# Conditioning sums of every second block on VectorE instead of TensorE, in a decoder layer

## The chip, the cores and the metric

The kernel runs on one core of a Trainium2 chip. The metric is the time of one execution on the device in microseconds; of several runs the median counts. The core has a matrix engine (TensorE, PE in the profile, with its weight loads listed as PEld), a vector engine (VectorE, DVE), a scalar engine (ScalarE, ACT), GpSimd (POOL) and a queue engine (SyncE, SP) that issues the transfers from memory here. Each engine takes its instructions in a fixed order and waits on semaphores for the others.

## The reference, cut to what matters

One decoder layer with two attention branches. The change touches only its beginning, the modulated norm and the first product with the input projection:

```
mod = silu(c) @ w_ada + b_ada                       # c: 1024 numbers, w_ada: 1024 x 3072
shift, scale, gate = split(mod, 3)
h = rms_norm(x, g_pre) * (1 + scale) + shift        # x: 256 tokens x 1024
proj = h @ w_in                                     # queries, keys, values and more
```

Behind it come two attentions, two output projections with gates, a merge, `w_out`, a second norm and the residual sum. They are the same before and after.

## The kernel before

Everything is in fp32, with 128 partitions. The 1024 channels are cut into eight blocks j = 0 to 7 of 128 channels. The first stage computes h of one block after the other (transposed, channels on partitions, tokens along the row) and at once multiplies it with the block's 128 rows of the input projection, 1536 columns, into six PSUM banks that collect over all eight blocks (two `acc` banks for queries, two `sc` for keys, two `pv` for values). For precision, h and the weights w are each split into a rounded part and a rest, and three products are formed: P0 = h1 w1, P1 = h2 w1, P2 = h1 w2. So each block has nine pairs of matmuls, P0q, P0k, P0v, P1q and so on, each pair for two tiles of 128 tokens.

To have h of block j, the kernel needs shift and scale of that block's 128 channels: a sum over all 1024 numbers of silu(c), with a slice of w_ada of 128 x 2048 numbers (8 slices k of 256 columns: 128 for shift, 128 for scale). The kernel makes it so:

- A (`ada_rows`, line 172): eight TensorE matmuls with a 32-column stationary operand (`scp`, silu(c) in its first column), that leave four rows of partial sums in the PSUM bank `bR` (tag `tr`). Behind them the slice's buffer `raw` is released, which lets SyncE issue the next load.
- E (`ada_evac`, line 181): ScalarE copies the 256 columns to SBUF (`rws`).
- T (`ada_cols`, line 185): two TensorE matmuls with `rws` and a column of ones sum over the partitions and turn the row into a column, again in `bR`.
- B (`ada_ab`, line 191): two tiny VectorE instructions make the factor and the offset per channel (`ab`).
- H and F (`h_act`, `h_full`): ScalarE writes h1 (rounded) and h in full; h (`h_low`): VectorE subtracts, giving h2.
- s and d: one split of a 128x512 piece of the weights; s is ScalarE's rounding copy, d is VectorE's subtraction `raw - w1`, three of each per block. The last d of a block releases the weights' `raw` buffer.

The order is written out by hand. The string `STEP` (line 44) lists, for the step of block j, the nine P of block j, and between them the letters above for block j+1 (s and d as well):

```
STEP = "s P0q P0k P0v P1q A d E s P1k P1v d P2q T B H F h s d P2k P2v"
```

`tokens` (line 368) walks through it, and `ordered` (line 77) ties each instruction to the one before it on its engine, so that for TensorE (key "T"), VectorE ("V") and ScalarE ("A") the program order in this stage is that of the string. `START` prepares block 0, `LAST` is the step of block 7. Five `raw` buffers go round; loads are issued in the fixed order of `LOADS` (line 36) by SyncE whenever a buffer is released. GpSimd builds the rotary tables meanwhile, from about 15 to 45 us.

Of the kernel before, what the change touches and what calls it, by code (L numbers as in the profile page):

```python
# [10 lines left out]
FT = mybir.dt.float32  # L11
# [3 lines left out]
OP = mybir.AluOpType  # L15
# [3 lines left out]
P = 128  # L19
D = 1024  # L20
S = 256
H = 8
KT = D // P
# [16 lines left out]

START = "A E T B H s F d h s d s d"
STEP = "s P0q P0k P0v P1q A d E s P1k P1v d P2q T B H F h s d P2k P2v"
LAST = "P0v P1v P2v V P0q P0k P1q P2q P1k P2k"
POOL_LOW = []

# [14 lines left out]
def hybrid_layer_kernel(ctx: ExitStack, tc: tile.TileContext, x, cols, pos, cst, gpost, bgate,  # L62
# [4 lines left out]
    wk = ctx.enter_context(tc.tile_pool(name="wk", bufs=2))  # L67
# [4 lines left out]
    V = nc.vector  # L72
# [4 lines left out]
    def ordered(eng, f, *a, **k):  # L77

        if eng in last_ins:
            with tc.issue_after(last_ins[eng]):  # L80
                r = f(*a, **k)  # L81
        else:
            r = f(*a, **k)
        last_ins[eng] = r.ins
        return r

    def bank(tag):
        return ps.tile([P, 512], FT, name=tag)
# [16 lines left out]
    raws, got, w1s, w2s = {}, {}, {}, {}  # L105
# [20 lines left out]
    sc = sb.tile([P, 8], FT, name="sc")  # L126
# [39 lines left out]

    ROW, COL = 0, 256
    rws = {}  # L170

# [9 lines left out]
    def ada_evac(j):  # L181
        rws[j] = wk.tile([P, 256], FT, name="rws", tag="acc", bufs=2)
        ordered("A", act, rws[j], bR[:, ROW:ROW + 256], AF.Copy)

    def ada_cols(j):
        r = rws.pop(j)
        for i in range(2):
            ordered("T", mm, bR[:, COL + 8 * i + j:COL + 1 + 8 * i + j], r[:, i * P:(i + 1) * P], ones[:, 0:1],
                    start=False, stop=True, skip_group_check=True)
# [47 lines left out]
    def pump():  # L237
        while loads and (loads[0] in ('p', 'm') or held[0] < RAW or loads[0][0] in raws):
            if loads[0] in ('p', 'm'):
                with tc.issue_after(dl[-1]):  # L240
                    dl.append((nc.sync.dma_start(post, pos) if loads.pop(0) == 'p' else nc.sync.dma_start(mask, cst[:, 160:])).ins)
                continue
            raw(*loads.pop(0))

    def release():
        held[0] -= 1
        pump()

    def split_one():
        if not splits:  # L250
            return False
        u, key, c0, a, b = splits[0]
        if key not in raws or got.get(key, 2048) < c0 + b:
            return False
        if a == 0:
            i = order.index(u)
            if i >= RING and order[i - RING] not in finished:
                return False
            w1s[u] = rg.tile([P, 1024], FR, name="w1", bufs=RING)
            w2s[u] = rg.tile([P, 1024], FR, name="w2", bufs=RING)  # L260
        splits.pop(0)
        r = raws[key][:, c0 + a:c0 + b]
        w = key[0] == "w"
        free = lambda eng, f, *a, **k: f(*a, **k)  # L264
        o = ordered if w else free
        if u == ("w", 0, 0) and a == 0:
            o("V", V.tensor_copy, w1s[u][:, a:b], r)
        else:
            o("A", act, w1s[u][:, a:b], r, AF.Copy)
        rel = key != ("gate",) and (not splits or splits[0][1] != key)  # L270
        if w:
            subs.append((u, key, a, b, r, rel))
            return True
        eng = "G" if (order.index(u), a // 512) in POOL_LOW else "V"
        free(eng, dict(V=V, G=G)[eng].tensor_tensor, w2s[u][:, a:b], r, w1s[u][:, a:b], op=OP.subtract)
        if rel:
            release()
        return True
# [3 lines left out]
    def sub_one():  # L282
        u, key, a, b, r, rel = subs.pop(0)
        ordered("V", V.tensor_tensor, w2s[u][:, a:b], r, w1s[u][:, a:b], op=OP.subtract)
        if rel:
            release()
# [27 lines left out]
        mm(bV[0][:, :P], ones, ones, start=True, stop=True)  # L314
    for t in range(2):
        act(scr, xs[:, t, :], AF.Square, accum_out=ss[:, t:t + 1])
    bR = bank("tr")
    for t in range(2):
        V.tensor_scalar(rs[:, t:t + 1], ss[:, t:t + 1], 1.0 / D, EPS, op0=OP.mult, op1=OP.add)
        pw = G.tensor_tensor(rs[:, t:t + 1], rs[:, t:t + 1], mhalf[:, 0:1], op=OP.pow)  # L320
# [2 lines left out]
        for g in range(2):  # L323
# [4 lines left out]
            dst, src = xnT[:, 4 * g:4 * g + 4, t * P:(t + 1) * P], b.rearrange("p (k n) -> p k n", k=4)  # L328
# [27 lines left out]
    def proj(j, which, lst, hard=True):  # L356
        for b, t, o, n, u in lst:
            w1, w2 = w1s["w", j, u], w2s["w", j, u]
            assert not any(x[0] == ("w", j, u) and x[3] < o + n and o < x[4] for x in splits)
            assert which < 2 or not any(x[0] == ("w", j, u) and x[2] < o + n and o < x[3] for x in subs)  # L360
            ha, wa = ((h1, w1), (h2, w1), (h1, w2))[which]
            m = (ordered if hard else lambda e, f, *a, **k: f(*a, **k))("T", mm, b[:, :n], ha[:, j, t * P:(t + 1) * P], wa[:, o:o + n],
                   start=(j == 0 and which == 0),
                   stop=(j == KT - 1 and which == 2), skip_group_check=True)
        return m.ins


    def tokens(j, toks):
        for t in toks.split():
            if t == "s":  # L370
                if splits[0][1][0] == "w":
                    assert split_one(), splits[0]
            elif t == "d":
                if subs:
                    sub_one()
            elif t[0] == "P":
                proj(j, int(t[1]), dict(q=accs[:2], k=accs[2:4], v=accs[4:])[t[2]])
            elif t == "V":
                vevac()
            elif j + 1 < KT:  # L380
                dict(A=ada_rows, E=ada_evac, T=ada_cols, B=ada_ab, H=h_act, F=h_full, h=h_low)[t](j + 1)

    tokens(-1, START)
    with tc.issue_after(pw.ins):
        rope_tables()
    for j in range(KT - 1):
        tokens(j, STEP)
        finished.update((("w", j, 0), ("w", j, 1)))
    vbt = sb.tile([P, 2, 512], FT, name="vbt", tag="vg")
    vb = [vbt[:, t] for t in range(2)]  # L390
# [2 lines left out]
    def vevac():  # L393
        for t in range(2):
            vlast.append(ordered("A", act, vb[t], bV[t], AF.Copy).ins)

    tokens(KT - 1, LAST)
    assert splits[0][1][0] != "w" and not subs and len(vlast) == 2
    finished.update((("w", KT - 1, 0), ("w", KT - 1, 1)))
# [547 lines left out]
```

## Time and profile before

| | |
|---|---|
| median of three runs | 235.46 us (233.86 to 235.47) |
| profiled execution, its own time | 236.85 us |
| its span, first to last instruction | 235.1 us |
| mean granted TensorE clock | 0.978 |
| TensorE busy | 223.1 us (95% of the span) |
| VectorE busy | 169.0 us (72%) |
| ScalarE busy | 134.7 us (57%) |
| GpSimd busy | 50.8 us (22%) |

A start in the timeline is in us from the span's start, then comes how long the instruction (or the run of like instructions, "x2") took. Matmuls in fp32 are pipelined, so a pair's time overlaps that of the next pair, and the distance between starts says more than the duration. In brackets stands how long the engine was idle before, and what ended the idle time. The granted clock is a share of 2.4 GHz: 1.00 is that, 0.50 is 1.2 GHz.

### The profile page before, as it was taken

To read this page: it belongs to the slowest core of one execution; us is meant where nothing else is said; L and a number is where in the kernel's file an instruction comes from. 1 tells how busy PE (TensorE), PEld (TensorE's weight loads), DVE (VectorE), ACT (ScalarE), POOL (GpSimd) and SP (SyncE) were. 2 spreads that over 40 slices of the span, in tenths; PEclk is the share of its full clock that TensorE was granted. 3 is DMA by queue.
4 is the path that set the end of the run, shared out by engine and by line. 5 is a ranking of instruction groups with operands and counts; after the bars stand their busy time and mean duration, and the time that the engine had idled before them with its cause. 6 is when DMAs were issued, how large, how long until landed. Compare 5 with 4: busy or idle time off the path is not lost.

```text
span 235.1 us, 4288 instructions
## 1 busy us (share of the span) xinstructions
PE 223.1 (95%) x1558; PEld 190.6 (81%) x1558; DVE 169.0 (72%) x415; ACT 134.7 (57%) x320; POOL 50.8 (22%) x82
## 2 busy tenths in 40 slices
PE   8679999999899999999999999999999999999990
PEld 8255666666699999999979988989999899988890
DVE  1462455444799767989979998999987566899543
ACT  4262444555866478649765996547477433664320
POOL 1138888500045101500000000000400000463000
PEclk9877999999999999999999999999999999999997
DMA  6999788898985534250550515789789720000022
GB/s 199 362 404 403 253 295 277 298 303 314 337 331 180 198 163 178 92 180 0 184 178 1 181 25 206 287 287 326 265 315 419 282 96 3 1 0 3 0 89 89
DMA packets 10679, 47.05 MB, mean 200 GB/s; under 512 B 1441, under 2 KB 2081, under 8 KB 7586
## 3 DMA queue, kind: packets, MB, share of 16 engines
q1 hardware_dynamic: 10658, 46.78, 55.5%
q8 instruction: 12, 0.20, 0.3%
q14 instruction: 9, 0.07, 0.1%
HBM read 45.73 MB, written 1.05 MB: 199 GB/s over the span
## 4 chain that ended last, share of the span: by engine, by line
PE 87%; DMA 3%; DVE 2%; issue 2%; ACT 1%; SPq 1%; POOLq 0%; POOL 0%; DVEq 0%; ACTq 0%
PE acc L417 9%; PE acc L419 9%; PE acc L418 9%; PE sc L81 6%; PE acc L81 5%; PE pv L81 5%; PE tr L81 5%; PE pv L686 3%; DMA raw<-in_wada_dram 3%; PE acc L745 3%; PE tr L676 2%; PE acc L747 2%; PE acc L746 2%; PE sc L653 2%; PE sc L645 2%
## 5 line engine op out<-in xcount | busy, mean ns | idle before, releaser
L264 ACT ACTIVATE w<-raw 128x512 fp32r<-128x512 f32 (+1 forms) x93 | 52.4, 617 | 34.3 <-PE acc L418 11.0
L264 DVE TENSOR_TENSOR w<-raw,w 128x512 fp32r<-128x512 f32 (+1 forms) x93 | 63.8, 727 | 6.2 <-ACT w L264 5.3
L417 PE MATMUL acc<-h,w 128*128 128x256 f32 x184 | 53.0, 288 | 0.1
L419 PE MATMUL acc<-h,w 128*128 128x256 f32 x184 | 52.8, 287 | 0.0
L418 PE MATMUL acc<-h,w 128*128 128x256 f32 x184 | 52.3, 284 | 0.0
L417 PEld LDWEIGHTS acc<-h,w 128*128 128x128 f32 x184 | 34.7, 188 | 1.2 <-issue 0.7
L419 PEld LDWEIGHTS acc<-h,w 128*128 128x128 f32 x184 | 34.7, 188 | 0.6
L418 PEld LDWEIGHTS acc<-h,w 128*128 128x128 f32 x184 | 34.7, 188 | 0.3
L81 DVE TENSOR_TENSOR w<-raw,w 128x512 fp32r<-128x512 f32 x24 | 16.8, 729 | 14.6 <-ACT w L81 14.2
L81 PE MATMUL acc<-w,h 128*128 128x512 f32 x48 | 16.1, 420 | 1.3 <-ACT h L81 1.3
L717 POOL TENSOR_TENSOR gacc<-gacc,bgt 1x1024 f32<-1x1024 f32 x1 | 2.6, 2570 | 67.7 <-PE acc L418 67.7
L81 PE MATMUL pv<-w,h 128*128 128x512 f32 x48 | 16.0, 418 | 1.0 <-ACT w L81 1.0
L81 PE MATMUL sc<-w,h 128*128 128x512 f32 x48 | 16.4, 426 | 0.3 <-ACT w L81 0.3
L757 POOL TENSOR_TENSOR y<-yy,y 128x256 fp32r<-128x256 f32 x8 | 8.5, 1074 | 37.3 <-ACT y L756 37.3
L665 ACT ACTIVATE p<-p,mx 128x128 f32<-128x128 f32 (+1 forms) x32 | 14.2, 445 | 0.1
L81 ACT ACTIVATE w<-raw 128x512 fp32r<-128x512 f32 x23 | 13.5, 618 | 0.0
L81 PEld LDWEIGHTS acc<-w,h 128*128 128x128 f32 x48 | 8.8, 194 | 5.5 <-ACT h L81 3.9
L81 PEld LDWEIGHTS pv<-w,h 128*128 128x128 f32 x48 | 8.6, 193 | 4.5 <-ACT w L81 3.2
L81 PEld LDWEIGHTS sc<-w,h 128*128 128x128 f32 x48 | 7.9, 189 | 4.6 <-issue 3.1
L443 POOL TENSOR_TENSOR rr<-rr,m 128x512 f32<-128x512 f32 x4 | 5.6, 1420 | 25.6 <-DVE m L442 25.6
L678 ACT ACTIVATE pT<-tr 128x384 f32<-128x384 f32 x16 | 7.7, 486 | 5.7 <-PE tr L676 5.6
L81 ACT ACTIVATE rws<-tr 128x256 f32<-128x256 f32 x7 | 2.7, 384 | 14.4 <-PE tr L81 14.4
(250 smaller groups left out, 529.8 us busy)
## 6 DMA issues: line engine op xcount, KB each, us to landing
raw<-in_win_dram SPq DMA_DIRECT2D x12, 1024.0 KB, 4.8
raw<-in_wada_dram SPq DMA_DIRECT2D x16, 512.0 KB, 6.1
raw<-in_win_dram SPq DMA_DIRECT2D x8, 512.0 KB, 6.6
raw<-in_wadag_dram SPq DMA_DIRECT2D x4, 1024.0 KB, 4.9
raw<-in_wo_dram SPq DMA_DIRECT2D x4, 1024.0 KB, 4.8
raw<-in_wout_dram SPq DMA_DIRECT2D x4, 1024.0 KB, 9.4
raw<-in_win_dram SPq DMA_DIRECT2D x8, 256.0 KB, 6.8
raw<-in_winl_dram SPq DMA_DIRECT2D x2, 832.0 KB, 6.3
```

The costliest lines, as they stand in the source:

```text
L81: r = f(*a, **k)
L264: free = lambda eng, f, *a, **k: f(*a, **k)
L417: mm(o, w1[:, k], h1[:, k], start=(k == 0), stop=False)
L418: mm(o, w1[:, k], h2[:, k], start=False, stop=False)
L419: mm(o, w2[:, k], h1[:, k], start=False, stop=(k == KT - 1))
L443: eng.tensor_tensor(dst, dst, m2, op=OP.add)
L645: mm(sct[i][:, 0:P], view(q0, i), view(k0, i), start=True, stop=True)
L665: act(p[:, a:e], p[:, a:e], AF.Exp, scale=scale, bias=mx[:, t:t + 1], accum_out=sm[:, t:t + 1])
L678: act(pT, b[:, :384], AF.Copy)
L686: mm(b[64 * i:64 * i + 64, 0:S], v[0][:, h * 64:h * 64 + 64], pTt[br, h][:, 0:S], start=True, stop=False, skip_group_check=True)
L745: mm(o, w1[:, k, c0:c0 + P], u1[br][:, k], start=(k == 0), stop=False)
L757: G.tensor_tensor(y2[:, m], yy, y1[:, m], op=OP.subtract)
```

## The change

For blocks 2, 4 and 6 the eight matmuls A and the copy E are dropped. Instead VectorE sums over k itself: eight instructions of 128x256, the first a product of a slice with silu(c) of its channels (a number per partition), the other seven a product added to the sum so far. The running sum stands in a PSUM bank of its own (`bC`, a second buffer of tag `tr`), the last instruction writes `rws` to SBUF. T then sums `rws` over the partitions as before. Block 0 and the odd blocks keep A and E.

The hand-written order now has two forms. The step of an even block (which prepares an odd one) is as before, with three tokens `c c c` behind its last d; each c is two of the eight instructions. The step of an odd block (which prepares an even one) begins with the fourth c, has no A and no E, and has T, B and H ahead of P2q. In step 6 the list of sums is used up and `c c c` does nothing.

```diff
-STEP = "s P0q P0k P0v P1q A d E s P1k P1v d P2q T B H F h s d P2k P2v"
+STEPS = ("s P0q P0k P0v P1q A d E s P1k P1v d P2q T B H F h s d c c c P2k P2v",
+         "s c P0q P0k d P0v P1q s P1k P1v d T B H P2q F h s d P2k P2v")
...
+    chain = [(j, n) for j in range(2, KT, 2) for n in range(4)]
+
+    def ada_pair(j, n):
+        r = raws["ada", j].rearrange("p (k n) -> p k n", k=KT)
+        assert got["ada", j] >= 512 * n + 512
+        a = bC[:, 0:256]
+        for k in (2 * n, 2 * n + 1):
+            dst = a
+            if k == KT - 1:
+                dst = rws[j] = wk.tile([P, 256], FT, name="rws", tag="acc", bufs=2)
+            if k == 0:
+                ordered("V", V.tensor_scalar, dst, r[:, k], sc[:, k:k + 1], None, op0=OP.mult)
+            else:
+                ordered("V", V.scalar_tensor_tensor, dst, r[:, k], sc[:, k:k + 1], a, op0=OP.mult, op1=OP.add)
+        if n == 3:
+            release()
...
-    bR = bank("tr")
+    bR, bC = bank("tr"), bank("tr")
...
+            elif t == "c":
+                if chain:
+                    ada_pair(*chain.pop(0))
...
-        tokens(j, STEP)
+        tokens(j, STEPS[j % 2])
```

Two places show what moves. The first is VectorE around the beginning of the step of block 5, which prepares block 6. Before (`h` is token h of step 4, w_512 its last d, the two w_522 the first two d of step 5, `ab` token B, what is in brackets is what the instruction waits for):

```order
L81 TENSOR_TENSOR h_163<-hf,h_162 128x256 [waits Activation_49]
L81 TENSOR_TENSOR w_512<-raw,w_511 128x512 [waits DMAHW4_49,Activation_49]
L81 TENSOR_TENSOR w_522<-raw,w_521 128x512 [waits DMAHW7_49,DVE_49,Activation_49]
L81 TENSOR_TENSOR w_522<-raw,w_521 128x512 [waits Activation_49]
L81 SCALAR_TENSOR_TENSOR ab<-tr,colt 128x1 [waits DVE_49,PE_49]
L81 TENSOR_TENSOR ab<-tr,colt 128x1
```

and in the change (w_511 is the last d of step 4, `tr` the new bank, w_527 the first two d of step 5):

```order
L83 TENSOR_TENSOR h_164<-hf,h_163 128x256 [waits Activation_49]
L83 TENSOR_TENSOR w_511<-raw,w_510 128x512 [waits DMAHW4_49,Activation_49]
L83 TENSOR_SCALAR tr<-raw,sc 128x256 [waits DMAHW5_49,DVE_49]
L83 SCALAR_TENSOR_TENSOR tr<-raw,sc,tr 128x256 [waits DVE_49] x3
L83 SCALAR_TENSOR_TENSOR tr<-raw,sc,tr 128x256 [waits DMAHW6_49,DVE_49]
L83 SCALAR_TENSOR_TENSOR tr<-raw,sc,tr 128x256 [waits DVE_49] x2
L83 SCALAR_TENSOR_TENSOR rws<-raw,sc,tr 128x256 [waits DVE_49]
L83 TENSOR_TENSOR w_527<-raw,w_526 128x512 [waits DMAHW7_49,Activation_49]
L83 TENSOR_TENSOR w_527<-raw,w_526 128x512 [waits Activation_49]
L83 SCALAR_TENSOR_TENSOR ab<-tr,colt 128x1 [waits PE_49]
```

All eight instructions stand in one piece between the last d of step 4 and the first d of step 5, ahead of both d and of `ab`.

The second is TensorE in the step of block 5. Before (w_468 is w1 of block 5 for queries and keys, w_511 for values, w_469 is w2; h_162 is h1, h_163 is h2; 32x256 is A, 128x1 is T):

```order
L81 MATMUL acc<-w_468,h_162 128x512 x2
L81 MATMUL sc<-w_468,h_162 128x512 x2
L81 MATMUL pv<-w_511,h_162 128x512 x2
L81 MATMUL acc<-w_468,h_163 128x512 x2
L81 MATMUL tr<-raw,scp 32x256 x8
L81 MATMUL sc<-w_468,h_163 128x512 x2
L81 MATMUL pv<-w_511,h_163 128x512 x2
L81 MATMUL acc<-w_469,h_162 128x512 x2
L81 MATMUL tr<-ones,rws 128x1 x2
L81 MATMUL sc<-w_469,h_162 128x512 x2
```

and in the change (w_467 and w_510 are w1 of block 5, w_468 is w2, h_163 is h1, h_164 is h2):

```order
L83 MATMUL acc<-w_467,h_163 128x512 x2
L83 MATMUL sc<-w_467,h_163 128x512 x2
L83 MATMUL pv<-w_510,h_163 128x512 x2
L83 MATMUL acc<-w_467,h_164 128x512 x2
L83 MATMUL sc<-w_467,h_164 128x512 x2
L83 MATMUL pv<-w_510,h_164 128x512 x2
L83 MATMUL tr<-ones,rws 128x1 x2
L83 MATMUL acc<-w_468,h_163 128x512 x2
L83 MATMUL sc<-w_468,h_163 128x512 x2
```

The eight matmuls A are gone, and T has moved from behind P2q to ahead of it. On GpSimd and SyncE the order is the same as before, and behind block 7 it is the same on every engine.

## Rows read from the trace of the kernel before

**Rows 1.** The page: shares of the chain of work that ended last.
```profile
PE 87%; DMA 3%; DVE 2%; issue 2%; ACT 1%; SPq 1%; POOLq 0%; POOL 0%; DVEq 0%; ACTq 0%
```

**Rows 2.** Windows of steps 1 to 6: busy us by engine, sum and mean.
```profile
sum 36.90, PE 36.90 PEld 24.07 DVE 17.59 ACT 18.24 POOL 18.75; mean PE 6.15 PEld 4.01 DVE 2.93 ACT 3.04 POOL 3.12
```

**Rows 3.** Timeline of TensorE in step 5: start, duration, engine, line, tile, count.
```profile
47.94 0.73 PE L81 MATMUL acc<-w,h 128*128 128x512 f32 x2
...
50.08 1.07 PE L81 MATMUL tr<-raw,scp 128*32 128x256 f32 x16
51.08 0.73 PE L81 MATMUL sc<-w,h 128*128 128x512 f32 x2
...
52.11 0.63 PE L81 MATMUL acc<-w,h 128*128 128x512 f32 x2
52.58 0.50 PE L81 MATMUL tr<-ones,rws 128*128 128x1 f32 x4
52.94 0.71 PE L81 MATMUL sc<-w,h 128*128 128x512 f32 x2
...
54.09 0.73 PE L81 MATMUL acc<-w,h 128*128 128x512 f32 x2
```

**Rows 4.** Timeline of VectorE: B, h and two d behind T of step 4.
```profile
46.97 0.22 DVE L81 SCALAR_TENSOR_TENSOR ab<-tr,colt 128x1 f32<-128x1 f32 x1 [0.20 <-PE tr L81]
47.10 0.15 DVE L81 TENSOR_TENSOR ab<-tr,colt 128x1 f32<-128x1 f32 x1
48.41 0.43 DVE L81 TENSOR_TENSOR h<-hf,h 128x256 fp32r<-128x256 f32 x1 [1.16 <-ACT hf L81]
48.93 1.29 DVE L81 TENSOR_TENSOR w<-raw,w 128x512 fp32r<-128x512 f32 x2
```

**Rows 5.** Timeline of ScalarE: H, F and two s behind T of step 4.
```profile
47.29 0.60 ACT L81 ACTIVATE h<-xnT,ab 128x256 fp32r<-128x256 f32 x1 [1.25 <-DVE ab L81]
47.79 0.59 ACT L81 ACTIVATE hf<-xnT,ab 128x256 f32<-128x256 f32 x1
48.28 1.14 ACT L81 ACTIVATE w<-raw 128x512 fp32r<-128x512 f32 x2
```

**Rows 6.** Timeline of VectorE elsewhere: like operations, with and without dependence.
```profile
88.90 0.41 DVE L428 SCALAR_TENSOR_TENSOR sz<-th,acc 128x256 f32<-128x256 f32 x1
...
72.19 1.40 DVE L442 TENSOR_TENSOR m<-sc,ssin 128x256 f32<-128x256 f32 x4
...
14.32 0.42 DVE L81 CAST w<-raw 128x512 fp32r<-128x512 f32 x1
14.77 0.69 DVE L81 TENSOR_TENSOR w<-raw,w 128x512 fp32r<-128x512 f32 x1
...
5.69 0.17 DVE L131 TENSOR_SCALAR sc<-sc 128x8 f32<-128x8 f32 x1
5.97 0.17 DVE L132 COPY scp<-sc 128x8 f32<-128x8 f32 x1
```

**Rows 7.** TensorE's timeline; windows (length, PE busy, PEclk, DMA share, GB/s).
```profile
15.15 0.73 PE L81 MATMUL acc<-w,h 128*128 128x512 f32 x2 [1.33 <-ACT h L81]
...
61.25 1.21 PE L81 MATMUL pv<-w,h 128*128 128x512 f32 x4 [0.98 <-ACT w L81]
...
16.00:17.00 1.00, 0.83 (x3) 0.82 1.01 399
17.00:18.00 1.00, 1.00 (x4) 0.50 1.05 418
...
19.00:20.00 1.00, 1.00 (x16) 0.50 1.02 393
...
61.00:62.00 1.00, 0.75 (x3) 1.00 0.90 377
```

**Rows 8.** SyncE's issue of block 4's weights; the page's landing time.
```profile
26.62 0.81 SPq L113 DMA_DIRECT2D raw<-in_win_dram  x2
...
raw<-in_win_dram SPq DMA_DIRECT2D x8, 512.0 KB, 6.6
```

## The prediction

> **What bounds the kernel now.** I read the page's shares first, then the windows by block, then the timeline of one block on each engine. The page's chain that ended last is 87% TensorE [rows 1], so the first question is whether the stage that is edited, the loop over blocks 1 to 6, is bound by TensorE too. The windows answer it: all six blocks take 6.15 us each, TensorE is busy for all of it, VectorE for 2.93 us on average [rows 2]. A microsecond of TensorE work taken out here would be a microsecond won, as long as nothing else becomes the last to arrive.
>
> What could become that is seen in the timeline. Take the step of block 5, which prepares block 6. P0q starts at 47.94, the rows A at 50.08, P1k at 51.08, the column sums T at 52.58, P2k at 52.94, P0q of the next block at 54.09 [rows 3]. Behind T hangs a short chain over three engines. In the step before, T starts 6.15 earlier than this one, at 46.43; VectorE's two `ab` instructions follow at 46.97 and 47.10, ScalarE's H at 47.29 for 0.60, and P0q starts at 47.94, 0.05 after H ends. After H come F (47.79), ScalarE's third copy `s` (48.28), VectorE's h (48.41) and its third subtraction `d` (48.93) [rows 3 to 5]. So TensorE is full, but the chain from T to the next P0q, 1.51 us, has almost no slack: P0q starts 0.05 behind H. Whoever delays T by a microsecond delays the next block.
>
> **What is removed.** In steps 1, 3 and 5 the eight A matmuls leave TensorE; they hold it from 50.08 to 51.08, 1.00 us [rows 3], so 3.0 us in all if nothing takes their place. The ScalarE copy E goes with them, on an engine with 3 us idle per block; it is worth nothing by itself. Moving T ahead of P2q puts one more pair (0.47, from 52.11 to 52.58) between T and the next P0q.
>
> **What is added, and where it stands.** Eight VectorE instructions of 128x256 per even block, all in front of the two `d` of the odd step, which stand in front of `ab`; VectorE takes them strictly in that order. Seven of the eight read what the one before wrote, and the order shows each waiting for VectorE's own semaphore. No instruction of the kernel before writes PSUM from VectorE, so the price is bounded by near rows. The same operation reading PSUM at this size lasts 0.41 us. Without a dependence such instructions overlap: four of 128x256 take 1.40, which is 0.41 and three starts 0.33 apart. With one they do not: a subtraction that waits for the cast ahead of it starts at 14.77, 0.03 after the cast's end (14.32 + 0.42). The widest gap of such a pair is 5.69 + 0.17 to 5.97, so 0.11 (0.53 between starts for 0.42) [rows 6]. The start-to-start pitch p is thus 0.33 (low), 0.53 (high); I take 0.41 + 0.03 = 0.44, because the order shows the wait.
>
> **The odd step, worked on the clock of rows 3 to 5.** The third `d` starts at 48.93 and the next instruction 1.29 - 0.69 = 0.60 later, so the first sum starts at 49.53. The eighth starts at 49.53 + 7p and lasts 0.41; T follows 0.05 behind. With p = 0.44 T starts at 53.07. TensorE would have been ready at 50.08 + 1.03 = 51.11 (P1k and P1v, from 51.08 to 52.11): it waits 1.96 us, twice what the removed rows gave back. Then come, on VectorE, the first `d` 0.33 after the eighth sum's start, the second 0.60 later, `ab` 0.60 later, the second `ab` 0.14 later for 0.15, H 0.04 later for 0.60, P0q 0.05 later. P0q of the next block starts at 49.53 + 7p + 2.51 = 52.04 + 7p = 55.12, against 54.09: **1.03 us later** for each of three odd steps. TensorE's own way from T (0.36 + 1.15 + 0.47 = 1.98, so 55.05) is shorter; it waits a little there too. The even steps are as before, from P0q on. Chain term: 3 x 1.03 = 3.1 us, with ends 3 x 0.26 = 0.8 (p 0.33) and 3 x 1.66 = 5.0 (p 0.53).
>
> **The clock.** A wait of 1.96 us in one piece is new in this stage, and the start of this trace shows what waits do. TensorE sat idle for 1.33 us up to 15.15; the granted clock then fell to 0.50, from 2.4 to 1.2 GHz, for part of one window and the whole of three. The 0.98 us up to 61.25 had no fall behind it [rows 7]. One fall costs 0.18 + 3 x 0.50 = 1.7 us of TensorE work; since part of it can lie in a wait, where it costs nothing, I take 1.5. The new wait is longer than the idle time ahead of that fall, but whether each of the three brings one can't be read from these rows; I count two: 3.0 us (ends 0 and 5.1).
>
> **Edits at nothing.** The raw buffer of block 6 comes free at 53.0, not 51.1, and the weight load behind it is issued 1.9 us later. Such a load was issued at 26.62 and lands after 6.6 us, at 33.2; it is first read by the first `s` of step 3, the second copy of the row at 48.28 taken two blocks (12.3) earlier, near 36.5 [rows 2, 5, 8]. The 3.3 us of slack cover 1.9, and the reading is later too. The second PSUM bank was free. Behind block 7 no engine's order is changed, and TensorE is the bound there, so the delay passes on whole.
>
> **Sum.** 3.1 + 3.0 = 6.1 us. On the profiled execution's own 236.85 that is 242.95; this execution lies 1.4 above the median of 235.46, so as a median 241.6.
>
> **A rule of the skill against my pitch.** The widest doubt in the sum is whether a dependent sum costs 0.44 or 0.33 [rows 6]. The Trainium skill, VectorE: DVE Perf Modes, section "The DRAIN you can't avoid", says that eight copies took the same time with a semaphore after each as with one behind the last, so by it the waits add nothing. The trace has both kinds of pair and disagrees for its small sample. By the rule the chain term would be 0.8.
>
> **Rivals.** *The clock holds*: T is late as worked out, but no fall follows, as none followed the 0.98 us; 235.46 + 3.1 = 238.6. *The sums overlap (not slower)*: p = 0.33, T waits 52.30 - 51.11 = 1.2, near the wait that had no fall; 235.46 + 0.8 = 236.3. It decides at 52.04 + 7p = 54.87 (a third of 1% of the time per odd step), p = 0.40: below it the median stays within 1%. *The rows' price is won (faster)*: all 3.0 us, 232.5; that needs P0q at 53.09, p = 0.15, under half of the lowest pitch in the trace; what speaks for it is only that VectorE is idle for half of each block. *Dear sums*: p = 0.53 and three falls, 5.0 + 4.5, 245.0; GpSimd works beside VectorE in two of the three odd steps.
>
> **Chances.** Forecast 0.47, the clock holds 0.27, sums overlap 0.13, dear 0.10, faster 0.03. A measurement of this kernel can tell about 1% (2.4 us) from no change. Slower by over 1% takes the forecast, the dear case and all but a little of the held clock: 0.82; within 1%: 0.15; faster 0.03. The range leaves out the faster case, most of the overlapping sums and half of the dear: 237.2 to 244.3. The likeliest one's own is 240 to 243.5.
>
> **What would show it.** In the changed trace: VectorE's sums in rows of eight, 0.44 apart; T waiting for `rws` of VectorE for about 2 us in steps 1, 3 and 5, and nowhere else; odd steps of some 7.2 us beside even steps of 6.15 where the clock is 1.00; slices at 0.50 between 27 and 65 us. I am wrong if the sums start under 0.40 apart, if T does not wait, if the even steps change at full clock, or if the time behind the last block changes.

## The result, and the profile after

The changed kernel takes 246.72 us as a median (244.63 to 247.31), the kernel before 235.47 beside it: slower by a factor of 1.045, 95% interval 1.040 to 1.051. That is 11.2 us more, on the side that was forecast and beyond the upper end of the range, 244.3. The ratios, here and below, leave out executions more than 1.5% above the fastest of their kernel; the medians keep them.

The page's first line and TensorE's clock, in 40 slices of the span:

```profile
span 244.5 us, 4213 instructions
...
PEclk9999798597699999999999999999999999999998
```

Three dips stand in the first twelve slices, where the edited stage lies. The windows of steps 1 to 5 in the changed kernel, cut at the starts of P0q (length, busy time of PE, PEld, DVE, ACT and POOL, then granted clock, DMA share, GB/s), answer to [rows 2]:

```profile
20.57:29.12 8.55, 5.89 (x23) 4.34 (x23) 6.62 (x15) 3.33 (x7) 7.09 (x18) 0.90 0.97 374
29.12:35.83 6.71, 6.71 (x40) 4.55 (x38) 2.71 (x6) 2.36 (x6) 5.71 (x12) 0.88 0.76 270
35.83:45.30 9.47, 6.73 (x24) 5.10 (x24) 7.40 (x16) 3.88 (x8) 6.95 (x13) 0.77 0.65 226
45.30:52.41 7.11, 7.11 (x39) 4.83 (x37) 2.03 (x5) 1.81 (x5) 0.00 (x0) 0.82 0.72 226
52.41:61.80 9.39, 6.72 (x23) 5.10 (x23) 7.32 (x16) 4.13 (x8) 0.00 (x0) 0.80 0.63 223
```

Every step was 6.15 us before. The odd steps (first, third, fifth line) now take 8.55, 9.47 and 9.39, and TensorE is idle for 2.7 us in each; the even ones take 6.71 and 7.11 with TensorE busy throughout, at a clock of 0.88 and 0.82. Both halves of the loss stand here: a wait, and a slower clock behind it. From the start of P0q of block 1 to the first product behind the last wait for `s` (70.19 - 20.57 = 49.62, against 61.25 - 23.34 = 37.91) it is 11.7 us. From there to the end it is 0.5 us, as one window of each kernel shows, the changed one first:

```profile
70.19:244.50 174.31, 167.95 (x1232) 153.45 (x1232) 142.56 (x356) 105.79 (x265) 23.19 (x20) 0.99 0.43 157
```

```profile
61.25:235.10 173.85, 167.63 (x1232) 153.35 (x1232) 142.59 (x356) 105.97 (x265) 23.23 (x20) 0.99 0.45 162
```

(The two spans differ by only 9.4 us because step 1 begins at 20.57 instead of 23.34: in this execution of the changed kernel the granted clock was 1.00 in every microsecond up to 20, where in the one of before it fell to 0.50 twice, from 10 to 13 and from 17 to 20 [rows 7]. The change has no part in that, since nothing ahead of step 1's beginning is edited on TensorE, and other edits of the changed kernel had the falls.)

Step 5 on TensorE, to be held against [rows 3]:

```profile
52.41 0.73 PE L83 MATMUL acc<-w,h 128*128 128x512 f32 x2
...
54.92 0.63 PE L83 MATMUL pv<-w,h 128*128 128x512 f32 x2
58.22 1.02 PE L83 MATMUL tr<-ones,rws 128*128 128x1 f32 x4 [2.67 <-DVE rws L83]
59.10 1.20 PE L83 MATMUL acc<-w,h 128*128 128x512 f32 x2
...
61.80 1.05 PE L83 MATMUL acc<-w,h 128*128 128x512 f32 x2
```

and on VectorE, to be held against [rows 4]:

```profile
53.41 0.69 DVE L83 TENSOR_TENSOR w<-raw,w 128x512 fp32r<-128x512 f32 x1
54.01 0.48 DVE L83 TENSOR_SCALAR tr<-raw,sc 128x256 f32<-128x256 f32 x1
54.53 3.12 DVE L83 SCALAR_TENSOR_TENSOR tr<-raw,sc,tr 128x256 f32<-128x256 f32 x6
57.68 0.48 DVE L83 SCALAR_TENSOR_TENSOR rws<-raw,sc,tr 128x256 f32<-128x256 f32 x1
58.08 1.29 DVE L83 TENSOR_TENSOR w<-raw,w 128x512 fp32r<-128x512 f32 x2
59.28 0.21 DVE L83 SCALAR_TENSOR_TENSOR ab<-tr,colt 128x1 f32<-128x1 f32 x1
```

A sum lasts 0.48 us and the next starts 0.52 after it (54.01 to 57.68 is seven starts, 3.67 us). TensorE waits for `rws` for 2.67 us, P2q then takes 1.20 where a pair took 0.63 to 0.73. The windows of one microsecond behind the wait (length, PE busy, granted clock, DMA share, GB/s) say why:

```profile
57.00:58.00 1.00, 0.00 (x0) 1.00 0.52 213
58.00:59.00 1.00, 0.78 (x4) 0.53 0.07 27
59.00:60.00 1.00, 1.00 (x4) 0.50 0.84 146
...
63.00:64.00 1.00, 1.00 (x4) 0.50 0.59 156
64.00:65.00 1.00, 1.00 (x4) 0.55 0.98 418
```

The clock is at 0.50, 1.2 GHz, from about 58 to 65. There are three such stretches, one behind each odd step's wait: the first costs 1.7 us of TensorE work, as the one in [rows 7] did; the second and third cost 3.4 each (seven windows wholly or partly slow instead of four).

### The profile page after: what moved, and what is told of

The parts are those of the page before. It is cut to its first block, busy times and chain, and to the rows that moved or that the text cites. A ratio compares the mean times of both kernels' runs of the same rounds, so it can differ in the third digit from the quotient of the medians.

```text
span 244.5 us, 4213 instructions
## 1 busy us (share of the span) xinstructions
PE 224.1 (92%) x1510; PEld 194.0 (79%) x1510; DVE 179.2 (73%) x439; ACT 133.5 (55%) x317; POOL 49.5 (20%) x82
## 4 chain that ended last, share of the span: by engine, by line
PE 76%; DVE 8%; DMA 6%; ACT 4%; issue 3%; SPq 1%; POOLq 0%; POOL 0%; DVEq 0%; ACTq 0%
PE acc L440 9%; PE acc L442 9%; PE acc L441 8%; DVE tr L83 4%; PE acc L83 4%; PE sc L83 4%; PE tr L83 3%; PE pv L83 3%; PE pv L709 3%; DMA raw<-in_wada_dram 3%; PE acc L768 2%; PE acc L769 2%; PE acc L770 2%; PE tr L699 2%; PE sc L676 2%
## 5 line engine op out<-in xcount | busy, mean ns | idle before, releaser
L83 PE MATMUL acc<-w,h 128*128 128x512 f32 x48 | 18.1, 467 | 1.3 <-ACT h L83 1.3
L83 PE MATMUL sc<-w,h 128*128 128x512 f32 x48 | 18.2, 469 | 0.3 <-ACT w L83 0.3
L83 PE MATMUL pv<-w,h 128*128 128x512 f32 x48 | 17.4, 451 | 1.0 <-ACT w L83 1.0
L83 ACT ACTIVATE h<-xnT,ab 128x256 fp32r<-128x256 f32 x8 | 4.8, 601 | 21.6 <-DVE ab L83 21.6
L83 PEld LDWEIGHTS acc<-w,h 128*128 128x128 f32 x48 | 10.3, 227 | 4.7 <-ACT h L83 2.6
L83 PEld LDWEIGHTS pv<-w,h 128*128 128x128 f32 x48 | 10.2, 220 | 4.6 <-ACT w L83 2.4
L83 PEld LDWEIGHTS sc<-w,h 128*128 128x128 f32 x48 | 9.9, 221 | 4.2 <-issue 1.6
L83 PEld LDWEIGHTS tr<-ones,rws 128*128 128x128 f32 x32 | 5.3, 224 | 9.7 <-DVE rws L83 9.4
```

## The experiments

All are edits of the changed kernel; each was timed beside the kernel before on the same chip, whose median there was 235.2 to 236.6.

**Which part is the chain and which the clock: keep TensorE busy while it waits.**

```diff
-         "s c P0q P0k d P0v P1q s P1k P1v d T B H P2q F h s d P2k P2v")
+         "s c P0q P0k d P0v P1q s P1k P1v x d T B H P2q F h s d P2k P2v")
...
+            elif t == "x":
+                if j + 2 < KT:
+                    for _ in range(20):
+                        ordered("T", mm, bR[:, ROW:ROW + 256], h1[:, j, 0:P], w1s["w", j, 0][:, 0:256], ...)
```

> The changed kernel, with 20 TensorE matmuls of 128x256 ahead of T in steps 1, 3 and 5, whose result nobody uses (they write the part of bR that A uses in the even steps). They are to fill about 2.1 of the 2.7 us that TensorE waits for the sums there; T itself comes no earlier. Theory A (the late sums cost 1.7 us per odd step and the rest is the clock that falls behind each wait): the granted clock stays at 1.00 from 20 to 65 us, TensorE waits under 0.8 us ahead of T, and the time is 235.5 + 5.5 = 241.0. Rival B (the slow stretches lie in waits and cost nothing, all 11 us are the chain from the sums to the next block): the clock stays up and the time remains at 246 to 247.

Measured: 241.96 us, a ratio of 1.024 (1.018 to 1.029). Twenty useless matmuls in each of three waits made the kernel 4.8 us faster by the medians; it is 5.4 us above the kernel before that was timed beside it, the changed kernel was 11.2 above. The windows of its steps 1 to 5, as above, and the start of step 6:

```profile
23.05:31.00 7.95, 7.64 (x43) 6.12 (x42) 6.46 (x14) 2.65 (x6) 6.59 (x17) 1.00 0.73 255
31.00:37.17 6.17, 6.16 (x39) 4.02 (x39) 3.34 (x6) 3.06 (x7) 5.40 (x10) 1.00 0.69 242
37.17:45.42 8.25, 7.59 (x44) 6.10 (x43) 6.75 (x14) 2.65 (x6) 6.89 (x14) 1.00 0.81 269
45.42:51.57 6.15, 6.15 (x38) 4.01 (x38) 2.70 (x6) 3.04 (x7) 0.00 (x0) 1.00 0.69 246
51.57:59.50 7.93, 7.63 (x44) 6.19 (x43) 6.33 (x14) 2.75 (x6) 0.00 (x0) 1.00 0.77 261
...
59.41 0.73 PE L83 MATMUL acc<-w,h 128*128 128x512 f32 x2
```

The clock is 1.00 in all of them, the even steps are back at 6.17 and 6.15, and the odd steps take 7.96, 8.25 and 7.84 (the last window was cut 0.09 behind the start of P0q). T still waits 0.3 to 0.4 us for the sums, so its time is the one that VectorE allows. What is left above 3 x 6.15 is 5.6 us: that is the chain alone, and theory A's 5.5 stands. Of the 11.7 us in the stage the other 6.1 go with the clock. Rival B, which had the slow stretches lie in waits only, is out. (The stretches cost 8.5 us of TensorE work, so 2.4 of it must have lain where TensorE would have waited anyway; that is a difference, not a reading.)

**Why a sum is dear: PSUM or the scalar per partition.** First, the running sum in SBUF:

```diff
-    bR, bC = bank("tr"), bank("tr")
+    bR = bank("tr")
+    bC = wk.tile([P, S], FT, name="u", bufs=2)
```

> The changed kernel, with the running sum in SBUF instead of a PSUM bank. Theory P (a sum is dear because VectorE reads and writes PSUM in it): the sums take 0.41 instead of 0.48 us, start 0.44 apart instead of 0.52, T comes 0.6 us earlier in each odd step, and the time is about 244. Rival S (the scalar per partition makes it dear, wherever the sum lies): the sums start 0.52 apart as before, and the time is 246 to 247.

Measured: 247.71 us, 1.046 (1.038 to 1.054), not faster and above both ranges. VectorE in step 5:

```profile
54.46 0.35 DVE L83 TENSOR_SCALAR u<-raw,sc 128x256 f32<-128x256 f32 x1
54.85 3.09 DVE L83 SCALAR_TENSOR_TENSOR u<-raw,sc,u 128x256 f32<-128x256 f32 x6
57.97 0.48 DVE L83 SCALAR_TENSOR_TENSOR rws<-raw,sc,u 128x256 f32<-128x256 f32 x1
```

Only the first instruction, a product alone, is quicker in SBUF (0.35 instead of 0.48); the seven that add last 0.48 and start 0.52 apart wherever the sum lies, here and in step 1. PSUM is not the reason. In step 3 the sums in SBUF were dearer still:

```profile
38.26 3.66 DVE L83 SCALAR_TENSOR_TENSOR u<-raw,sc,u 128x256 f32<-128x256 f32 x6
```

They start 0.62 apart there, and TensorE waits 3.50 us ahead of T instead of 2.74. GpSimd works beside VectorE at that time, but so it does in step 1; the cause was not looked for. Then the constant 0.5 for the scalar per partition:

```diff
-                ordered("V", V.scalar_tensor_tensor, dst, r[:, k], sc[:, k:k + 1], a, op0=OP.mult, op1=OP.add)
+                ordered("V", V.scalar_tensor_tensor, dst, r[:, k], 0.5, a, op0=OP.mult, op1=OP.add)
```

(and the same in the first of the eight).

> The changed kernel, with the constant 0.5 in place of the scalar per partition in the eight sums; this leaves out the weighting with silu(c) for blocks 2, 4 and 6. Theory S (the scalar per partition makes a sum dear): the sums take 0.41 instead of 0.48 us and start 0.44 apart instead of 0.52; T comes 0.6 us earlier in each odd step, the wait ahead of it falls to 2.0 us, and the time is 243 to 245. Rival P (PSUM makes it dear): 0.48 and 0.52 as before, 246 to 247.

Measured: 242.76 us, 1.028 (1.021 to 1.035). VectorE in step 5:

```profile
54.36 0.42 DVE L83 TENSOR_SCALAR tr<-raw 128x256 f32<-128x256 f32 x1
54.81 2.74 DVE L83 SCALAR_TENSOR_TENSOR tr<-raw,tr 128x256 f32<-128x256 f32 x6
57.59 0.42 DVE L83 SCALAR_TENSOR_TENSOR rws<-raw,tr 128x256 f32<-128x256 f32 x1
```

Now they last 0.42 and start 0.46 apart. The scalar read per partition costs 0.06 us in each. The time fell a little more than expected, to 0.2 us under the range. In the profiled execution (243.02 us) one wait of 2.2 us had no slow stretch behind it, which may be the reason. The windows behind the first, second and third wait in this kernel:

```profile
31.00:32.00 1.00, 1.00 (x4) 0.50 0.83 320
...
45.00:46.00 1.00, 1.00 (x4) 0.50 0.84 287
...
59.00:60.00 1.00, 1.00 (x6) 1.00 0.87 186
```

The waits were 2.16, 2.25 and 2.17 us; the clock fell behind two of them.

**What the wait for the sum just ahead costs.** Two running sums, of even and of odd k, at first both in the one bank:

```diff
+            a = bC[:, 256 * (k % 2):256 * (k % 2) + 256]
...
+            if k == KT - 2:
+                two[j] = wk.tile([P, 256], FT, name="rw2", tag="u", bufs=2)
+                dst = two[j]
```

(T adds `rws[j]` and `two[j]` with four matmuls.)

> The changed kernel with two running sums, of even and of odd k, so that a sum never reads what the one just ahead of it wrote; T adds both with four matmuls instead of two. Theory D (the wait for the sum ahead costs 0.1 us a piece, as rows 6 have it): the sums last 0.48 as before but start 0.40 to 0.42 apart, T comes 0.7 to 0.8 us earlier in each odd step, and the time is 3 to 5 us under that of the changed kernel, 242 to 244. Rival W (the waits add nothing, by the Trainium skill, VectorE: DVE Perf Modes, section The DRAIN you can't avoid): they start 0.52 apart as before, and the time is 246 to 247.

Measured: 245.80 us, 1.048 (1.041 to 1.056), and this run doesn't tell the theories apart as planned. Both halves lie in one tile, and the sums still start as if each waited for the one just ahead; only the last does not, which reads a half of the bank while the one ahead of it writes to SBUF:

```profile
56.03 2.06 DVE L83 SCALAR_TENSOR_TENSOR tr<-raw,sc,tr 128x256 f32<-128x256 f32 x4
58.13 0.48 DVE L83 SCALAR_TENSOR_TENSOR rw<-raw,sc,tr 128x256 f32<-128x256 f32 x1
58.52 0.47 DVE L83 SCALAR_TENSOR_TENSOR rws<-raw,sc,tr 128x256 f32<-128x256 f32 x1
```

It starts 0.39 behind the one ahead, the others 0.52 apart. So one of the sums was moved to SBUF, where it is a tile of its own:

```diff
+            a = (bC[:, 0:256], uC)[k % 2]
...
+    uC = wk.tile([P, 256], FT, name="uC", tag="th", bufs=2)
```

> Again two running sums of even and of odd k, now in two places (one in the PSUM bank, one in SBUF), since in e5_two both halves lay in one bank and each sum still waited for the one just ahead. Theory D (a wait for the instruction just ahead adds 0.12 us): the sums last 0.48 and start 0.40 apart, the eighth ends about 0.8 us earlier after the first than in the changed kernel, TensorE waits 1.9 us ahead of T, and the time is 242 to 244.5. Rival W (the waits add nothing): 0.52 apart and 246 to 247.

Measured: 242.55 us, 1.026 (1.017 to 1.034). The profiled execution was the longest of the five, 246.95 us; so the length of its steps is not read, but how VectorE's sums follow one another, and the waits ahead of T (1.86, 1.82 and 1.61 us where 1.9 was expected). The last four of the eight in step 5:

```profile
58.21 0.48 DVE L83 SCALAR_TENSOR_TENSOR tr<-raw,sc,tr 128x256 f32<-128x256 f32 x1
58.61 0.48 DVE L83 SCALAR_TENSOR_TENSOR uC<-raw,sc,uC 128x256 f32<-128x256 f32 x1
59.00 0.47 DVE L83 SCALAR_TENSOR_TENSOR rw<-raw,sc,tr 128x256 f32<-128x256 f32 x1
59.39 0.48 DVE L83 SCALAR_TENSOR_TENSOR rws<-raw,sc,uC 128x256 f32<-128x256 f32 x1
```

Same duration, 0.39 apart. The wait for the instruction just ahead costs 0.13 us per sum. That the two sums lie in different places is not the reason: the last pair of the run with one bank, both reading the bank and writing to SBUF, started 0.39 apart too. By the Trainium skill, VectorE: DVE Perf Modes, section "The DRAIN you can't avoid", a semaphore after each of eight copies cost nothing extra. Here the measurement decides against such a rule, for this operation and size.

**Whether it is the place: the same sums spread out.** Two pairs go to the middle of the even step, behind E, where VectorE waited for `s`; one between `ab` and h, where it waited for F; the last stays:

```diff
-STEPS = ("s P0q P0k P0v P1q A d E s P1k P1v d P2q T B H F h s d c c c P2k P2v",
+STEPS = ("s P0q P0k P0v P1q A d E c c s P1k P1v d P2q T B c H F h s d P2k P2v",
```

> The changed kernel with another place for the sums: two of the four pairs in the middle of the even step behind E, one between ab and h, and the last where it was, at the head of the odd step. No operation is added or left out. Theory A (the price is their place, all eight in a row ahead of T): TensorE waits under 0.3 us ahead of T in the odd steps, the odd steps take 5.1 to 5.4 us, the even ones 6.15, the clock holds, and the time is 235.5 - 3.0 = 232.5 (at worst 234). Rival C (VectorE hasn't the time, wherever the sums lie): they push d and ab back in the even steps, which become longer than 6.5 us, and the time is 236 or more.

Measured: 232.64 us, 0.983 (0.976 to 0.990) of the kernel before. No instruction is added or taken away against the changed kernel, only moved, and 11 us became a gain. The profiled execution, the longest of the four (235.34 us), had a wait left. VectorE and TensorE in step 4 and at its end:

```profile
42.95 0.49 DVE L83 TENSOR_SCALAR tr<-raw,sc 128x256 f32<-128x256 f32 x1 [1.06 <-DMA raw<-in_wada_dram]
...
46.48 0.73 PE L83 MATMUL acc<-w,h 128*128 128x512 f32 x2 [0.89 <-ACT h L83]
```

The sums of block 6 start so early now that they met their load. To see what that costs, the spread order was run for blocks 2 and 4 alone, beside a second run for all three:

```diff
-    chain = [(j, n) for j in range(2, KT, 2) for n in range(4)]
+    chain = [(j, n) for j in range(2, 6, 2) for n in range(4)]
...
-        tokens(j, STEPS[j % 2])
+        tokens(j, STEPS[j % 2] if j < 4 else STEPS[0])
```

> The spread order of e4_spread for blocks 2 and 4 only; block 6 keeps A and E on TensorE and ScalarE. In e4_spread the loads of block 6 came late (VectorE waited 1.1 us for them, TensorE 0.9 behind it). Theory L (the third block's microsecond was lost to the late load): no such wait, and the same time as e4_spread within 0.5 us, that is 2 us under the kernel before. Rival: each block moved is worth its 1.0 us whatever the load does, and this kernel is 0.8 us or more slower than e4_spread.

> The spread order of e4_spread for blocks 2, 4 and 6 once more, for a narrower interval, beside the version with two blocks. Theory A (place): 2 to 3 us under the kernel before, with the odd steps at 5.0 to 5.4 us. Rival: the first result was in part the luck of the clock at the start of the kernel, and the difference is under 1%.

Measured: 233.33 us with two blocks, 0.994 (0.991 to 0.997); 232.37 us with three, 0.990 (0.986 to 0.994), both against 235.19. Two blocks are worth 1.9 us, three 2.8, so 0.9 to 1.0 per block, near the 1.0 us that the rows A hold TensorE. The spread of these runs alone leaves 0.2 to 1.7 us between the two versions. The profiles are clearer: from P0q of block 1 to the first product behind the last wait for `s` (37.91 us before) it is 35.39 us with two blocks and 34.07 with three, so the third block brings its part, and theory L falls. Both stages are shorter by more than 1.0 us per block; with three blocks some of it was lost again behind the stage, where TensorE waited for ScalarE once, at 160.7 us, for 0.64 (1.17 in the first run's profile), a wait that neither the kernel before nor the version with two blocks has. So that the times come to 1.0 us per block is in part chance. The late load stands in the first of the two profiles only; in the second run's the sums of block 6 wait for none. The first comparison had shown a gain of 1.7%, this one with more runs shows 1.0% (0.6 to 1.4): part of the first result was chance, as the rival had it, though a gain remains. The second run's windows of steps 1 to 5:

```profile
23.00:27.82 4.82, 4.82 (x23) 3.75 (x23) 3.78 (x9) 2.73 (x6) 4.06 (x10) 1.00 0.76 252
27.82:33.90 6.08, 6.08 (x40) 3.94 (x39) 5.23 (x12) 2.97 (x7) 5.14 (x12) 1.00 0.98 334
33.90:39.05 5.15, 4.99 (x23) 3.62 (x22) 4.19 (x9) 2.65 (x6) 4.55 (x8) 1.00 0.89 304
39.05:45.20 6.15, 6.15 (x38) 4.01 (x38) 5.29 (x12) 3.04 (x7) 4.69 (x10) 1.00 0.90 304
45.20:50.03 4.83, 4.83 (x24) 3.81 (x23) 3.64 (x9) 2.79 (x6) 0.00 (x0) 1.00 0.99 378
```

The odd steps are 4.82 to 5.15 us, two of them shorter than expected; TensorE is busy in them but for 0.16 us, and the clock stays at 1.00. This version beats both kernels, the one before by 1.0%.

## Why the prediction was right in direction and wrong in size

**Bound and place: right.** TensorE set the pace, and T was late because eight sums stand in one piece ahead of it. The two rivals on the other side needed sums 0.40 and 0.15 us apart or less; they came 0.52 apart. The even steps are unchanged at full clock (6.17 and 6.15 with the filled wait), the loads cost nothing, and 0.5 us came or went behind block 7. That the sums' place did it, and not their number, is shown by the spread order.

**The price of a sum: wrong row.** The step "the same operation reading PSUM at this size lasts 0.41 us" took `sz` [rows 6], whose scalar is a constant. The sums have a scalar per partition, and the trace of before had that form at this very size, near the end of the kernel:

```profile
L860 DVE SCALAR_TENSOR_TENSOR ygt<-ygt,r,xr 128x256 f32<-128x256 f32 x1 | 0.5, 480 | 0.0
```

480 ns, and the new sums take 0.48 us. The doubt about PSUM, on which the bounds were spent, was beside the point; the doubt about the wait was decided the right way (0.03 to 0.04 behind the end of the one ahead). With 0.48 + 0.04 the prediction's own formula gives 52.04 + 7 x 0.52 = 55.68, so 1.59 per odd step and 4.8 in all, where the filled wait shows 5.6 and 3.1 was forecast. The last 0.8 lie on VectorE: in step 3 the two `d` behind the sums take 1.62 instead of 1.29 and the one ahead of them 0.1 longer too, in step 1 the two take 1.41, and the eighth sum holds VectorE for 0.40 where 0.33 was counted. GpSimd works beside VectorE in steps 1 and 3 and not in step 5; that this makes the `d` longer is likely, but was not tested. The path was right: with the clock at 1.00 the next P0q starts 0.05 behind the end of H in all three odd steps, so it is VectorE's chain and not TensorE's own way from T that ends last.

**The clock: right in kind, half in size.** Two falls of 1.5 us were counted, 3.0 us; there were three, two of them twice as long as the one from which the price was taken, and they cost 6.1. The failed step is the price, taken from one short fall as if all were of its kind, and then the count. That a wait need not bring a fall was right: the run with a constant scalar shows two in three, and so does the one with two sums in one bank. The "dear" rival, 0.53 apart and three falls, has the pitch and the number right and gave 245.0 with a chance of 0.10; it too had each fall at 1.5.

**The range** ended at 244.3 because the dear case was cut in half, and both mis-sized terms pointed the same way. It would be easy to say that they hang together, a longer sum making a longer wait and a longer wait a more certain fall. The runs don't show that. The longest wait in the run with two sums in one bank had no fall behind it, as its row and the window behind it show, while its waits of 2.53 and 2.52 us had one:

```profile
45.04 0.38 PE L83 MATMUL tr<-ones,rws 128*128 128x1 f32 x2 [2.73 <-DVE rws L83]
...
46.00:47.00 1.00, 1.00 (x6) 1.00 0.94 250
```

In the one profile of the run with sums in two places all three waits, of 1.6 to 1.9 us, had one. Which wait of this stage brings a fall, and whether a short or a long one, stays open.

## What to carry to other kernels

Before work is moved from the engine that sets the pace to one with idle time, look at where that idle time lies: the same eight instructions per block cost 11 us in one piece ahead of the thing that waits for them, and won 2.8 us in the gaps where the engine stood idle anyway. Price an instruction by a row of the same operation with the same kind of scalar, not only of the same shape, and a chain of sums by its dependent pairs. And count a wait on TensorE twice where the trace shows the clock falling behind such waits: once as time, once as the slow stretch behind it.

## What was not expected of the hardware

- Matmuls whose result nobody reads, put in a wait of TensorE, made the kernel 4.8 us faster, since the granted clock then stayed at 1.00 through the stage.
- The stretches at 1.2 GHz were of two lengths: 1.7 us of TensorE work lost at the first, 3.4 at the second and third, with TensorE busy through nearly all of them. The two long ones began while TensorE still waited, so that T's matmuls already ran at the slow clock (1.01 and 1.02 us, against 0.61 ahead of the short one). That isn't a rule: in the run with a constant scalar a short stretch, of 1.7 us, caught T as well (0.88). What decides the length wasn't found.
- A scalar read per partition adds 0.06 us to a VectorE sum of 128x256 (0.48 against 0.42), and a wait for the instruction just ahead 0.13 us (0.52 between starts against 0.39); the place of the running sum, PSUM or SBUF, adds nothing to it in steps 1 and 5 (in step 3 the sums in SBUF started 0.62 apart). To a product alone it does: 0.48 into PSUM, 0.35 into SBUF in the same two steps.
